# A decoder layer on one core: each weight unit ordered behind x's high part of the same rows, and the pre-norm's mean two rows later

## The chip, the cores and the metric

The kernel runs on one core of a Trainium2 chip. The metric is device microseconds of one launch; a kernel's time is the median of its runs.

## The reference

One decoder layer is applied to 288 tokens (256 of a prompt and 8 x 4 of a sample), with d_model 2048, d_ff 5632 and fp32 data:

```python
x = x + 0.5 * rmsnorm(swiglu(rmsnorm(x, g[0]), ffn1_w_in, ffn1_w_out), g[1])
m, sg, sh = hybrid_mixer(rmsnorm(x, g[2]), mix_w_in, ...)   # GLA heads and HGRN2 heads, with states
x = x + rmsnorm(m, g[3])
x = x + 0.5 * rmsnorm(swiglu(rmsnorm(x, g[4]), ffn2_w_in, ffn2_w_out), g[5])
```

`rmsnorm(x, w)` is `x * rsqrt(mean(x*x) + 1e-6) * w`. The layer's time lies in the products with the weights: `swiglu` has two, the mixer an input and an output projection.

## The kernel before

Activations are kept transposed: `x[k]` is a tile of 128 features (row k of 16, called a row below) by 288 tokens. The program goes through three stages: the first FFN, the mixer, the second FFN. Each starts with a pre-norm (`pre1`, `pre2`, `pre3`). The norm's factor per token, `rt`, is not put on x but on the results of the products, when they are taken out of PSUM; so the products can start before `rt` is known.

**Products in three parts.** A number is split into a high part in fp32r and the rest. For x that is `xh` (ScalarE, L272) and `xl` (VectorE, L273); for the weights `wh` (ScalarE, L101) and `wl` (VectorE, L102). A product is three matmuls: xh by wh (L550), xl by wh (L551), xh by wl (L552).

**Weight units.** The object `W` goes through the weights in units of 128 x 1024: two rows k, 2j and 2j+1, by 512 columns. SyncE loads them into `RAW_BUFS = 3` raw buffers (L74), 512 KB each, in order, so the load of unit i waits until `wl` of unit i-3 is done with its buffer. Split units lie in `HL_BUFS = 4` pairs of wh and wl; a pair is free when the matmuls of its unit are done. `W.ahead` splits units as far as there is room. If `W.behind` holds instructions, the next call of `ahead` orders its units behind them:

```python
            behind, self.behind = self.behind, None
            with ExitStack() as es:
                for ins in behind:
                    es.enter_context(self.tc.issue_after(ins))
                self.ahead(most)
            return
```

The order on each engine is set when the program is built, by a scheduler; `issue_after` gives it an instruction that has to stand earlier. On the chip each engine works through its list.

**Blocks.** `block(name, ...)` computes 512 output columns as four tiles of 128 features (`qk0_0` to `qk0_3`), over 16 rows. For each row it issues 12 matmuls and then calls `tick(k)`; after each unit it calls `W.ahead`. At the end each tile is taken out of its PSUM bank by `evac`. A stage's first two blocks are `gate1_0` and `up1_0` in stage 1, `qk0` and `v0` in stage 2, `gate2_0` and `up2_0` in stage 3. `tick0` of the pre-norm runs in the first block, `tick1` in the second.

**Between stages.** A post-norm's `update(k)` makes the new x of row k: y[k] times the post-norm's factor (L523), x[k] from it (L524), then xh[k] and xl[k]. Rows 0 to 7 are updated before the first block of stages 2 and 3 (`UPDATED = 8`), rows 8 to 15 by `tick0` in it, row k+8 at row k. For stage 1 `made` is given and x comes from the input. Some of row products of tile 0 are made ahead from the old x and y apart (`Fill`) and are added at the end of that tile: `fsum` L509 scales them, L512 adds them to the bank of `qk0_0`, which is free afterwards.

**The mean.** `tick1` squares x (ScalarE, L408) and adds the squares up in `acc` (VectorE, L412). At one row it calls `rstd`: a matmul of `acc` with a constant matrix (`pre`, L439), a square root on ScalarE (L179) and a reciprocal on VectorE (L441), which gives `rt`. Behind them come a few instructions on `gate` and the functions of `late`: in the mixer the scaling of q and k by `rt` (L1545) and the small weights `a32`; in stage 3 that of the gates by `rt` (L611). The first tiles of `v0` are multiplied by `rt` at L910 and L911. `a_lr` (L1555) is a small product of x with `a32`, scaled by `rt` at L1556 on VectorE, and its result goes into the matmuls `zp` (L1562), which stand some matmuls into the next block.

In stage 2 GpSimd also loads the recurrent states `s` (L1245), 256 KB each, while the first block runs.

## Time and profile before

| | us |
|---|---|
| median of 3 runs | 2261.44 |
| lowest, highest | 2260.63, 2262.22 |
| the profiled execution | 2260.56 |
| its span | 2258.8 |
| TensorE busy in it | 2244.1 |
| VectorE, ScalarE busy | 1361.7, 1005.1 |

The profile is of one execution. The span runs from its first to its last instruction; what the execution takes beyond it, 1.8 us, lies around it. Stage 2 begins near 860 us of the span, stage 3 near 1400. A row of a timeline gives start and duration, engine, line, operation, output and inputs by name without buffer numbers, and in brackets the idle time ahead with what ended it. Consecutive rows of one kind may be joined (x2), and matmuls overlap, so their starts are what counts.

### The profile page before, as it was taken

The numbers are of one execution on the slowest core, as the hardware profiler recorded it, in microseconds if no ns is written. First come the engines' busy times: TensorE is split into PE (matmuls) and PEld (weight loads), VectorE is DVE, ScalarE is ACT, GpSimd is POOL, SyncE is SP. The second block draws the span as 40 slices with busy tenths as digits, with TensorE's granted clock in tenths as the row PEclk, the third lists the DMA queues.
The fourth block names the chain that finished last, engine by engine and source line by source line (L and its number), as shares of the span: only waits on it lengthen the run. The fifth ranks groups of instructions, "written<-read, shape, count | busy, mean of one in ns | idle before, by whom it ended". The sixth has DMA issues, their size and how long they took to land. (4 is left out here: it accounts for less than half of the span.)

```text
span 2258.8 us, 41337 instructions
## 1 busy us (share of the span) xinstructions
PE 2244.1 (99%) x17073; PEld 2226.7 (99%) x17073; DVE 1361.7 (60%) x2164; ACT 1005.1 (44%) x1508; POOL 78.3 (3%) x143
## 2 busy tenths in 40 slices
PE   9999999999999999999999999999999999999998
PEld 9999999999999999999999999999999999999998
DVE  7545545554565468778888745744555455545554
ACT  6443333333334344545566644543333333333345
POOL 0000000000000003022110000100000000000000
PEclk9999999999999999999999999999999999999999
DMA  7555555555555555466565654555555555555553
GB/s 218 163 167 168 164 166 166 168 165 165 166 168 180 168 166 162 135 208 204 173 171 162 184 178 128 170 163 165 169 168 162 166 167 160 168 167 160 167 168 109
DMA packets 207107, 377.94 MB, mean 167 GB/s; under 512 B 15411, under 2 KB 40801, under 8 KB 206913
## 3 DMA queue, kind: packets, MB, share of 16 engines
q1 hardware_dynamic: 198608, 356.83, 52.3%
q0 software_dynamic: 5984, 17.97, 2.5%
q8 instruction: 135, 2.21, 0.4%
q10 hardware_dynamic: 2320, 0.44, 0.1%
q14 instruction: 60, 0.48, 0.1%
HBM read 363.39 MB, written 11.80 MB: 166 GB/s over the span
## 5 line engine op out<-in xcount | busy, mean ns | idle before, releaser
L102 DVE TENSOR_TENSOR wl<-raw,wh 128x1024 fp32r<-128x1024 f32 (+1 forms) x674 | 822.0, 1220 | 643.9 <-ACT wh L101 641.3
L101 ACT ACTIVATE wh<-raw 128x1024 fp32r<-128x1024 f32 (+1 forms) x673 | 710.6, 1057 | 1054.5 <-PE gate L551 313.2
L550 PE MATMUL gate<-xh,wh 128*128 128x288 f32 x1660 | 487.7, 297 | 0.0
L552 PE MATMUL gate<-xh,wl 128*128 128x288 f32 x1660 | 487.5, 295 | 0.0
L551 PE MATMUL gate<-xl,wh 128*128 128x288 f32 x1660 | 487.4, 295 | 0.0
L551 PE MATMUL out<-hl,wh 128*128 128x288 f32 x1408 | 415.9, 295 | 0.0
L550 PE MATMUL out<-hh,wh 128*128 128x288 f32 x1408 | 415.4, 295 | 0.0
L552 PE MATMUL up<-xh,wl 128*128 128x288 f32 x1408 | 415.2, 295 | 0.0
L552 PE MATMUL out<-hh,wl 128*128 128x288 f32 x1408 | 415.1, 295 | 0.0
L551 PE MATMUL up<-xl,wh 128*128 128x288 f32 x1408 | 415.0, 295 | 0.0
L550 PE MATMUL up<-xh,wh 128*128 128x288 f32 x1408 | 414.6, 294 | 0.0
L551 PEld LDWEIGHTS gate<-xl,wh 128*128 128x128 f32 x1660 | 311.5, 188 | 0.9 <-DVE xl L273 0.5
L552 PEld LDWEIGHTS gate<-xh,wl 128*128 128x128 f32 x1660 | 311.2, 188 | 0.0
L550 PEld LDWEIGHTS gate<-xh,wh 128*128 128x128 f32 x1660 | 310.2, 188 | 0.9 <-ACT xh L272 0.5
L552 PEld LDWEIGHTS out<-hh,wl 128*128 128x128 f32 x1408 | 264.8, 188 | 0.0
L550 PEld LDWEIGHTS out<-hh,wh 128*128 128x128 f32 x1408 | 264.7, 188 | 0.0
L551 PEld LDWEIGHTS out<-hl,wh 128*128 128x128 f32 x1408 | 264.6, 188 | 0.0
L552 PEld LDWEIGHTS up<-xh,wl 128*128 128x128 f32 x1408 | 264.3, 188 | 0.1
L551 PEld LDWEIGHTS up<-xl,wh 128*128 128x128 f32 x1408 | 264.2, 188 | 0.1
L550 PEld LDWEIGHTS up<-xh,wh 128*128 128x128 f32 x1408 | 264.2, 188 | 0.1
L680 DVE TENSOR_TENSOR y<-out,y 128x288 f32<-128x288 f32 x288 | 121.6, 453 | 104.1 <-PE out L552 101.3
L550 PE MATMUL hfq<-xh,wh 128*128 128x288 f32 x256 | 78.0, 305 | 0.0
(373 smaller groups left out, 2395.8 us busy)
## 6 DMA issues: line engine op xcount, KB each, us to landing
raw<-in_ffn_w_in_dram SPq DMA_DIRECT2D x351, 512.0 KB, 3.7
raw<-in_ffn_w_out_dram SPq DMA_DIRECT2D x176, 512.0 KB, 3.7
raw<-in_mix_w_in_dram SPq DMA_DIRECT2D x64, 512.0 KB, 3.7
raw<-in_mix_w_in_dram SPq DMA_DIRECT2D x96, 256.0 KB, 3.4
raw<-in_mix_w_out_dram SPq DMA_DIRECT2D x32, 512.0 KB, 3.7
out_dram<-s POOLq DMA_DIRECT2D x32, 256.0 KB, 3.4
s<-in_state_gla_dram POOLq DMA_DIRECT2D x16, 256.0 KB, 4.3
s<-in_state_hgrn_dram POOLq DMA_DIRECT2D x16, 256.0 KB, 4.7
```

Source lines behind the costliest of these rows:

```text
L101: i1 = self.nc.scalar.activation(h[:, c], raw[:, c], AF.Copy).ins
L102: i2 = self.nc.vector.tensor_tensor(l[:, c], raw[:, c], h[:, c].bitcast(F32), op=ALU.subtract).ins
L550: yield lambda: PE.matmul(dst, w[0][:, c:c + P], parts[0], start=start, stop=False)
L551: yield lambda: PE.matmul(dst, w[0][:, c:c + P], parts[1], start=False, stop=False)
L552: yield lambda: PE.matmul(dst, w[1][:, c:c + P], parts[0], start=False, stop=stop)
L680: V.tensor_tensor(y[k], ps, y[k], op=ALU.add)
```

## The change

In stages 2 and 3, where `made` is None, `tick0` hands `xh` of the row just updated to `W.behind`. The next `W.ahead`, one in two rows, then orders the units that it splits behind it: behind xh9, xh11, xh13 and xh15 at the latest rows of the pairs. And in all three stages `tick1` calls `rstd` with all that follows at row 11 instead of 9. The number of lines grows by two above L455, so L550 of before is L552 after.

```diff
         def tick0(self, k):
             if k + self.ahead < KT:
                 self.split = self.update(k + self.ahead)
+                if self.made is None:
+                    W.behind = self.split[:1]
 
         def tick1(self, k):
...
-            if k == 9:
+            if k == 11:
                 ins = rstd(rt, (acc,), self.name)
```

Each engine issues the same instructions as before; what moves is their order. Names carry the unit or row number, and behind an underscore a running number of the build.

ScalarE in stage 2, in the first block, from xh11 on; wh are the weight units, sq the squares. Before:

```order
L272 ACTIVATE xh11_141<-x11_109,prm_94 128x288
L101 ACTIVATE wh272_9487<-raw272_9359 128x1024
L272 ACTIVATE xh12_142<-x12_110,prm_94 128x288
L272 ACTIVATE xh13_143<-x13_111,prm_94 128x288
L101 ACTIVATE wh273_9517<-raw273_9391 128x1024
L272 ACTIVATE xh14_144<-x14_112,prm_94 128x288
L272 ACTIVATE xh15_145<-x15_113,prm_94 128x288
L408 ACTIVATE acc_164<-x0_98 128x288
L101 ACTIVATE wh274_9550<-raw274_9429 128x1024
L408 ACTIVATE sq_9618<-x1_99 128x288
```

And after:

```order
L272 ACTIVATE xh11_141<-x11_109,prm_94 128x288
L101 ACTIVATE wh270_9387<-raw270_9153 128x1024
L272 ACTIVATE xh12_142<-x12_110,prm_94 128x288
L272 ACTIVATE xh13_143<-x13_111,prm_94 128x288
L101 ACTIVATE wh271_9425<-raw271_9236 128x1024
L101 ACTIVATE wh272_9487<-raw272_9359 128x1024
L272 ACTIVATE xh14_144<-x14_112,prm_94 128x288
L101 ACTIVATE wh273_9517<-raw273_9391 128x1024
L272 ACTIVATE xh15_145<-x15_113,prm_94 128x288
L408 ACTIVATE acc_164<-x0_98 128x288
L408 ACTIVATE sq_9618<-x1_99 128x288
L408 ACTIVATE sq_9633<-x2_100 128x288
```

wh269 to wh271 have moved down by several rows behind xh9, xh11 and xh13 (before, they stood ahead of xh7). xh14 and xh15 were both behind wh273; now xh14 stands ahead of it, xh15 behind it, and wh274 comes after two squares.

VectorE at the same place: before, from y9 to wl270, the low half of the unit whose buffer raw273 is loaded into next.

```order
L523 TENSOR_TENSOR y9_123<-y9_123,post1s_9277 128x288
L102 TENSOR_TENSOR wl269_9356<-raw269_9122,wh269_9355 128x1024
L273 SCALAR_TENSOR_TENSOR xl7_153<-x7_105,prm_94,xh7_137 128x288
L273 SCALAR_TENSOR_TENSOR xl8_154<-x8_106,prm_94,xh8_138 128x288
L524 SCALAR_TENSOR_TENSOR x9_107<-y9_123,hg1_95,x9_107 128x288
L523 TENSOR_TENSOR y10_124<-y10_124,post1s_9277 128x288
L523 TENSOR_TENSOR y11_125<-y11_125,post1s_9277 128x288
L273 SCALAR_TENSOR_TENSOR xl9_155<-x9_107,prm_94,xh9_139 128x288
L524 SCALAR_TENSOR_TENSOR x10_108<-y10_124,hg1_95,x10_108 128x288
L524 SCALAR_TENSOR_TENSOR x11_109<-y11_125,hg1_95,x11_109 128x288
L102 TENSOR_TENSOR wl270_9388<-raw270_9153,wh270_9387 128x1024
```

And after, from wl269 to wl270:

```order
L102 TENSOR_TENSOR wl269_9356<-raw269_9122,wh269_9355 128x1024
L273 SCALAR_TENSOR_TENSOR xl10_156<-x10_108,prm_94,xh10_140 128x288
L526 SCALAR_TENSOR_TENSOR x11_109<-y11_125,hg1_95,x11_109 128x288
L525 TENSOR_TENSOR y12_126<-y12_126,post1s_9277 128x288
L525 TENSOR_TENSOR y13_127<-y13_127,post1s_9277 128x288
L273 SCALAR_TENSOR_TENSOR xl11_157<-x11_109,prm_94,xh11_141 128x288
L526 SCALAR_TENSOR_TENSOR x12_110<-y12_126,hg1_95,x12_110 128x288
L102 TENSOR_TENSOR wl270_9388<-raw270_9153,wh270_9387 128x1024
```

Between wl269 and wl270 stood eight rows and now six, but wl269 itself stands seven rows lower, so wl270 has xl10, xl11, y12, y13 and x12 ahead of it in addition. Further down on VectorE, wl274 stood between the two rows of `fsum` and now stands behind them.

TensorE and ScalarE at the mean of stage 2, in the block v0. TensorE before:

```order
L552 MATMUL v0_1_9602<-xh10_140,wl277_9682 128x288
L550 MATMUL v0_2_9603<-xh10_140,wh277_9681 128x288
L439 MATMUL pre2_9798<-acc_164,onesD_89 128x288
L551 MATMUL v0_2_9603<-xl10_156,wh277_9681 128x288
L552 MATMUL v0_2_9603<-xh10_140,wl277_9682 128x288
```

TensorE after:

```order
L553 MATMUL v0_3_9604<-xl11_157,wh277_9681 128x288
L554 MATMUL v0_3_9604<-xh11_141,wl277_9682 128x288
L439 MATMUL pre2_9829<-acc_164,onesD_89 128x288
L552 MATMUL v0_0_9601<-xh12_142,wh278_9724 128x288
L553 MATMUL v0_0_9601<-xl12_158,wh278_9724 128x288
```

The mean stood within row 10 and now stands between rows 11 and 12. ScalarE before:

```order
L408 ACTIVATE sq_9761<-x14_112 128x288
L408 ACTIVATE sq_9764<-x15_113 128x288
L101 ACTIVATE wh280_9854<-raw280_9685 128x1024
L179 ACTIVATE rt_162<-pre2_9798,epst_91 128x288
L172 ACT_TABLE_LOAD
```

ScalarE after:

```order
L408 ACTIVATE sq_9761<-x14_112 128x288
L101 ACTIVATE wh280_9798<-raw280_9685 128x1024
L408 ACTIVATE sq_9764<-x15_113 128x288
L101 ACTIVATE wh281_9885<-raw281_9728 128x1024
L179 ACTIVATE rt_162<-pre2_9829,epst_91 128x288
```

Here wh281 stood behind the square root and now stands ahead of it; on VectorE, wl281 stands ahead of the reciprocal in the same way, where wl280 was the last before it. In stage 3 ScalarE and VectorE move alike.

## The prediction

> **What bounds it.** I read the page first, then the waits of TensorE, then each wait in the timeline of the engines.

> ```profile
> span 2258.8 us, 41337 instructions
> ...
> PE 2244.1 (99%) x17073; PEld 2226.7 (99%) x17073; DVE 1361.7 (60%) x2164; ACT 1005.1 (44%) x1508; POOL 78.3 (3%) x143
> ...
> PEclk9999999999999999999999999999999999999999
> ```

> TensorE is busy for 2244.1 of 2258.8 us, and its clock stays in the top tenth. The change adds and drops no matmul, so all it can give is idle time: 14.7 us in the whole kernel. It touches three waits by name:

> ```profile
> PE qk L550 <- ACT xh L272: 1.6, 1, 1.6
> ...
> PE v L550 <- DVE fsum L512: 0.8, 1, 0.8
> ...
> PEld qk L551 <- DVE xl L273: 0.2, 1, 0.2
> ```

> and the waits of the pre-norm means on `acc`, shown below. The timeline of TensorE around the first two (start, duration, line, operation, idle before it and its releaser):

> ```profile
> 880.65 0.30 PE L551 MATMUL qk<-xl,wh 128*128 128x288 f32 x1
> 880.78 0.29 PE L552 MATMUL qk<-xh,wl 128*128 128x288 f32 x1
> 882.63 0.80 PE L550 MATMUL qk<-xh,wh 128*128 128x288 f32 x4 [1.56 <-ACT xh L272]
> ...
> 887.13 0.29 PE L552 MATMUL v<-xh,wl 128*128 128x288 f32 x1
> 888.18 0.40 PE L550 MATMUL v<-xh,wh 128*128 128x288 f32 x1 [0.76 <-DVE fsum L512]
> ```

> Matmuls start 0.13 us apart, so these two gaps lose 882.63 - 880.78 - 0.13 = 1.72 and 888.18 - 887.13 - 0.13 = 0.92. ScalarE and VectorE tell why:

> ```profile
> 881.10 1.06 ACT L101 ACTIVATE wh<-raw 128x1024 fp32r<-128x1024 f32 x1 [4.19 <-PE qk L552]
> 882.06 0.94 ACT L272 ACTIVATE xh<-x,prm 128x288 fp32r<-128x288 f32 x2
> ...
> 885.45 1.06 ACT L101 ACTIVATE wh<-raw 128x1024 fp32r<-128x1024 f32 x1 [2.11 <-DMA raw<-in_mix_w_in_dram]
> ```
> ```profile
> 886.54 1.23 DVE L102 TENSOR_TENSOR wl<-raw,wh 128x1024 fp32r<-128x1024 f32 x1 [1.48 <-ACT wh L101]
> 887.68 0.45 DVE L512 TENSOR_TENSOR fsum<-fsum,qk 128x288 f32<-128x288 f32 x1
> ```

> The row at 881.10 is wh273, at 882.06 xh14 and xh15, at 885.45 wh274. xh14 waited behind wh273, and the residual sum L512 behind wl274. For wh273 the profile names TensorE, but the DMA came last:

> ```profile
> L74 SPq DMA_DIRECT2D raw<-in_mix_w_in_dram x1: 367/367/367, 874.0 to 874.0; - x1
> DMA to landing us min/median/max: 7.0/7.0/7.0
> ...
> L74 SPq DMA_DIRECT2D raw<-in_mix_w_in_dram x1: 368/368/368, 877.6 to 877.6; - x1
> DMA to landing us min/median/max: 7.8/7.8/7.8
> ```
> ```profile
> L1245 POOL DMA_DIRECT2D s<-in_state_gla_dram x7: 704/716/727, 871.4 to 875.7; - x7
> DMA to landing us min/median/max: 3.3/5.5/8.6
> ```
> ```profile
> 876.00:882.00 6.00, 5.07 (x39) 4.84 (x37) 5.26 (x9) 1.81 (x3) 6.00 (x22) 1.00 0.93 314
> ```
> ```profile
> raw<-in_ffn_w_in_dram SPq DMA_DIRECT2D x5, 512.0 KB, 3.6
> ```

> raw273 (issued 874.0) took 7.0 us and raw274 7.8, among seven state loads of 256 KB; the row of 876 to 882 (length, busy us of PE, PEld, DVE, ACT and POOL, PE clock, DMA share, GB/s) has the DMA engines 93% busy at 314 GB/s. The same loads at the third stage's start, without state loads (last row), take 3.6.

> **The change, step by step: stage 2 (mixer).** ScalarE used to take wh269 to wh273 as their buffers allowed; now they stand behind xh9, xh11, xh13 (two) and xh14. VectorE's wl units follow, and each raw load waits for the wl three units earlier, so loads go out later:

> ```profile
> 870.66 0.81 DVE L523 TENSOR_TENSOR y<-y,post1s 128x288 f32<-128x288 f32 x2
> ...
> 871.82 0.94 DVE L524 SCALAR_TENSOR_TENSOR x<-y,hg,x 128x288 f32<-128x288 f32 x2
> 872.68 1.22 DVE L102 TENSOR_TENSOR wl<-raw,wh 128x1024 fp32r<-128x1024 f32 x1
> 873.81 0.94 DVE L273 SCALAR_TENSOR_TENSOR xl<-x,prm,xh 128x288 fp32r<-128x288 f32 x2
> ```

> wl270 (872.68) now has xl10, xl11, y12, y13 and x12 ahead of it as well: two L523 (0.8), three of 0.43 (1.3), together 2.1. So raw273 is issued at about 876.1 instead of 874.0. Its landing L is the unknown: 876.1 + 3.6 = 879.7 if the engines are free, 876.1 + 7.8 = 883.9 if it fares as raw274. I take 881.8, the middle, and a count of bytes gives the same: the loads up to raw273 are those of before, landed by 881.0, except that about 0.25 MB of raw272 used to move before the state loads began; that is 0.8 us at 314 GB/s.

> Now xh14 no longer stands behind wh273, but xh15 does. TensorE would come to xh15 seven matmuls after xh14, at 880.78 + 8 x 0.13 = 881.8. Before, landing to resumption took 882.63 - 881.0 = 1.6 (wh273, then the xh), and does again: TensorE resumes at L + 1.6. The old waits (1.72 + 0.92, and 0.2 for the low half xl7, which wl269 used to hold up) give 2.84; the second cannot return as it was, since the sum L512 now stands ahead of wl274. The gain is Q = 2.84 - (L + 1.6 - 881.6) = 882.8 - L, hence **1.0** at 881.8, between -1.1 (883.9) and, if nothing waits, 2.84.

> **The later mean.** Before, TensorE waited for the last `acc`:

> ```profile
> 903.39 0.29 PE L550 MATMUL v<-xh,wh 128*128 128x288 f32 x1
> 904.32 0.72 PE L439 MATMUL pre<-acc,onesD 128*128 128x288 f32 x2 [0.63 <-DVE acc L412]
> 904.67 0.51 PE L551 MATMUL v<-xl,wh 128*128 128x288 f32 x1
> ...
> 1440.67 0.72 PE L439 MATMUL pre<-acc,onesD 128*128 128x288 f32 x2 [0.47 <-DVE acc L412]
> ```
> ```profile
> 54.03 0.29 PE L552 MATMUL up<-xh,wl 128*128 128x288 f32 x1
> ...
> 54.67 0.38 PE L550 MATMUL up<-xh,wh 128*128 128x288 f32 x1
> ```

> Stages 2 and 3 lose 0.63 and 0.47; stage 1 passes its mean in 54.67 - 54.03 = 0.64 with no wait. Behind row 11 the mean comes 17 matmuls later in stage 2 and 20 in stage 3, over 2 us, so both waits go: **-0.63, -0.47**. But everything on `rt` comes later too, and in stage 2 a consumer was just in time:

> ```profile
> 905.65 1.95 DVE L441 RECIPROCAL rt<-rt 128x288 f32<-128x288 f32 x1
> ...
> 909.70 1.23 DVE L102 TENSOR_TENSOR wl<-raw,wh 128x1024 fp32r<-128x1024 f32 x1
> ...
> 911.30 0.42 DVE L910 TENSOR_TENSOR y<-v,rt 128x256 f32<-128x256 f32 x1 [0.26 <-PE v L552]
> ...
> 915.87 0.45 DVE L1556 TENSOR_TENSOR y<-a_lr,rt 128x288 f32<-128x288 f32 x1
> ```
> ```profile
> 913.59 2.15 PE L1555 MATMUL a_lr<-x,a 128*32 128x288 f32 x32
> ...
> 916.42 1.19 PE L1562 MATMUL zp<-y,y 128*128 128x288 f32 x4
> ```

> Let E be the end of row 11 on TensorE. ScalarE now has wh281 ahead of the square root (0.96) and VectorE wl281 behind it, ahead of the reciprocal (1.13): with 0.15 for handing over, the reciprocal starts at E + 2.25. From it to L1556 went 915.87 - 905.65 = 10.2; wl281 (1.13) and the idle 0.26 drop out, two short instructions on `lb` come in (0.2): 9.0. With 0.55 from L1556 to zp, zp can start at E + 11.8. TensorE gets there after the mean (0.64), rows 12 to 15 (48 x 0.133 = 6.4) and the stretch from a_lr to zp (916.42 - 913.59 = 2.8): E + 9.9. This is a new wait of **+1.9** at zp, where none stood. Its bounds: 0 if VectorE's chain has slack that I don't see, 3.0 if it holds one wl unit (1.13) more than counted. Stage 2 sums to -1.0 - 0.63 + 1.9 = +0.3.

> **Stage 3 and stage 1.** In stage 3 ScalarE and VectorE move in the same way, but a load takes 3.6 us, so wh417 is not late: I take -0.47 for the mean and -0.2 for the low half behind the early weight unit (as in stage 2), with 0 to +0.6 for banks that are freed later because `rt` is (half of the wl unit of 1.13 that now stands ahead of the reciprocal). Consumers of `rt` there, as in stage 1, are evacuations after the whole row 15; the order moves the first matmuls of the block that reuses the bank six places back, which covers 0.8 of it. Stage 1 gets no new weight order: 0, at most +0.6.

> **Sum**: +0.3 - 0.7 + 0 = -0.4 us against the profiled execution's 2260.56, that is 2260.2. The runs' median, 2261.44, lies 0.9 above it: **2261.0**.

> [...]

> **Rivals.**
> - *All removed waits pay.* raw273 lands by 880.2 and zp does not wait: 2.84 + 0.63 + 0.47 + 0.2 = 4.1 less, 2257.3. For it: the load asks for what others no longer need at 880. Against it: 93% busy engines, and the VectorE row above. Chance 0.07.
> - *The load comes late, slower.* raw273 is now asked for in the thick of the state loads, and xh15 stands behind it. At L = 883.9 Q is -1.1, and the sum +1.7: 2263.1. It makes the kernel slower from L = 882.2 on, and by 0.2% only from 887. For it: 7.8 for the neighbour, 8.6 for a state load. Chance 0.2.
> - *rt too late everywhere.* If banks in stages 1 and 3 wait too, 0.6 each by the bound above: 2262.2. It speaks for it that zp had no slack, against it that evacuations there follow row 15. Chance 0.17.
> - *The clock drops.* A gap at xh15 (L + 1.6 less 881.6, so 3.9 us at 883.9) makes TensorE idle long enough that some matmuls run slower: at half the clock for as long as the gap, 2 us more, 2265.1. Against it: the gap of 1.85 from 880.78 left the clock of 876 to 882 at 1.00, in the row of that stretch. Chance 0.03. [...]

> **Numbers.** My forecast has 0.53. About 0.2% (4.5 us) is what a measurement can tell from no change here. Of all cases only the first with something on top ends faster by that (0.03), and the late load or the clock with another loss slower (0.04); 0.93 stays within. The range runs from 2258.5, with Q at 2.84 and two thirds of the zp wait, to 2263.4, just beyond the late load.

> **What would show it.** TensorE's waits should no longer list fsum L512 nor acc L412 at the means; a wait of qk on xh L272 of 1 to 3 us should stand at xh15 near 883, with wh L101 released by the DMA ahead of it; a wait of zp L1564 on y L1558 (new line numbers) of about 2 us should be new near 917. No wait at zp, or none at xh15, would each prove its step wrong. A total beyond 2266 would mean a wait in stages 1 or 3 that I have not seen, or a lower clock.

## The result and the profile after

The changed kernel is slower: 2266.93 us (median of 14 runs, 2263.96 to 2268.80) against 2262.59 for the kernel before in the same sets of runs (14 runs, 2260.57 to 2265.28). The ratio is 1.0018, 95% interval 1.0011 to 1.0026, so 4.3 us. That is just inside the 0.2% to which the chances were given, but on the other side than forecast, and beyond the range's upper end of 2263.4. Two launches among the runs below, 2710.38 us of the weight order alone and 2408.93 us of the kernel with 24 filling matmuls, had a granted clock of 0.75 and 0.85 and are left out of the ratios.

The waits of TensorE in the changed kernel's profile (line, releaser, us in total, times, longest):

```profile
PE qk L552 <- ACT xh L272: 3.4, 1, 3.4
...
PE zp L1564 <- DVE y L1558: 1.4, 1, 1.4
PE sc L1356 <- DVE Qv L1311: 0.9, 2, 0.6
PE pre L439 <- DVE acc L412: 0.3, 1, 0.3
```

The wait on fsum is gone, the means' waits have shrunk to 0.3, and zp waits anew, all as forecast. But the wait on xh has grown from 1.6 to 3.4. TensorE's timeline at that place, and behind it the stretches of 4 us from 880 to 896 (length, busy us and count of PE, PEld, DVE, ACT, POOL, PE clock, DMA share, GB/s):

```profile
883.29 0.30 PE L553 MATMUL qk<-xl,wh 128*128 128x288 f32 x1
883.43 0.29 PE L554 MATMUL qk<-xh,wl 128*128 128x288 f32 x1
887.07 0.85 PE L552 MATMUL qk<-xh,wh 128*128 128x288 f32 x2 [3.35 <-ACT xh L272]
887.72 0.44 PE L553 MATMUL qk<-xl,wh 128*128 128x288 f32 x1
887.96 0.44 PE L554 MATMUL qk<-xh,wl 128*128 128x288 f32 x1
```
```profile
880.00:884.00 4.00, 3.72 (x29) 3.48 (x27) 3.96 (x6) 1.74 (x3) 4.00 (x13) 1.00 1.01 333
884.00:888.00 4.00, 0.93 (x4) 0.93 (x5) 0.95 (x2) 2.46 (x6) 4.00 (x10) 0.71 0.81 249
888.00:892.00 4.00, 4.00 (x18) 4.00 (x18) 2.71 (x5) 1.60 (x3) 2.48 (x7) 0.50 0.55 147
892.00:896.00 4.00, 4.00 (x30) 4.00 (x30) 2.76 (x6) 0.74 (x2) 0.00 (x0) 0.94 0.52 144
```
```profile
882.25:885.66 3.41, 1.47 (x12) 1.23 (x10) 1.71 (x3) 0.12 (x1) 3.41 (x9) 1.00 0.98 296
885.67:892.48 6.81, 5.41 (x22) 5.41 (x23) 4.14 (x8) 4.36 (x7) 4.81 (x12) 0.50 0.57 169
```

Behind the gap matmuls start 0.24 apart instead of 0.13, and the granted clock is 0.50: 18 matmuls in 4 us where 30 are usual. The last two rows show the edges: the recorded clock is 1.00 up to 885.66 and 0.50 from there to 892.49. 21 steps of 0.24 in a row, each 0.107 too long, cost 2.2 us. Busy time counts them as work: TensorE's grew from 2244.1 to 2248.3 us.

ScalarE and the load of raw273 show whose wait it was:

```profile
881.23 0.52 ACT L272 ACTIVATE xh<-x,prm 128x288 fp32r<-128x288 f32 x1
885.54 1.06 ACT L101 ACTIVATE wh<-raw 128x1024 fp32r<-128x1024 f32 x1 [3.79 <-DMA raw<-in_mix_w_in_dram]
886.50 0.52 ACT L272 ACTIVATE xh<-x,prm 128x288 fp32r<-128x288 f32 x1
```
```profile
L74 SPq DMA_DIRECT2D raw<-in_mix_w_in_dram x1: 368/368/368, 878.0 to 878.0; - x1
...
DMA to landing us min/median/max: 7.4/7.4/7.4
```

The load of wh273 was issued at 878.0 and took 7.4 us; xh15 stood behind it.

To compare kernels, the same matmul is looked up in both traces and its start is subtracted; the table gives how the median difference to the first profile of the kernel before grows over each stretch (positive is slower; times are those of the kernel before). "Opening" is 855 to 895, "mean" to 908, "zp" to 925, "rest of mixer" to 1300, "stage 3" from 1398 to 1456.

| kernel | opening | mean | zp | rest of mixer | stage 3 |
|---|---|---|---|---|---|
| before, again | -0.2 | 0.0 | 0.0 | +0.4 | 0.0 |
| changed | +3.0 | -0.4 | +1.6 | +0.4 | -0.2 |
| changed, again | +3.3 | -0.4 | +3.6 | +1.8 | -0.7 |
| weight order alone | +2.3 | -0.1 | +1.2 | +0.3 | +0.5 |
| mean at row 11 alone | -0.2 | -0.9 | +2.1 | +0.7 | -0.4 |
| mean at row 10 alone | +0.8 | -0.7 | 0.0 | +0.2 | -0.7 |
| mean at row 10 alone, again | +0.7 | -0.7 | 0.0 | +0.4 | -0.7 |
| 24 filling matmuls | +2.4 | -0.9 | +3.6 | +1.4 | -0.7 |
| 12 filling matmuls | +1.3 | -0.9 | +2.1 | +3.0 | -0.7 |
| small state loads | -2.3 | -0.4 | +1.7 | +5.1 | -0.7 |
| units past xh15, mean at 10 | -1.6 | -0.4 | +1.1 | -0.1 | -0.2 |
| one unit held, mean at 10 | 0.0 | -0.7 | 0.0 | +0.1 | -0.7 |
| one held behind the sum too | -2.9 | +0.3 | +1.0 | +1.1 | -0.7 |

Ahead of the opening no kernel differs but by the start of the program: in the first profile of before the clock came up early, and most later profiles lost 1.5 to 2.2 us there, the changed kernel's among them (the last section shows it). Of the span's growth from 2258.8 to 2265.2, 2.2 us are of that kind and not the change's; the stretches of the changed kernel sum to +4.4.

### The profile page after: what moved, and what is told of

It reads as the page before. It is cut to its first block, busy times and chain, and to the rows that moved or that the text cites. A ratio compares the mean times of both kernels' runs of the same rounds, so it can differ in the third digit from the quotient of the medians.

```text
span 2265.2 us, 41340 instructions
## 1 busy us (share of the span) xinstructions
PE 2248.3 (99%) x17073; PEld 2230.4 (98%) x17073; DVE 1361.4 (60%) x2164; ACT 1006.6 (44%) x1508; POOL 77.1 (3%) x143
## 5 line engine op out<-in xcount | busy, mean ns | idle before, releaser
L102 DVE TENSOR_TENSOR wl<-raw,wh 128x1024 fp32r<-128x1024 f32 (+1 forms) x674 | 821.5, 1220 | 646.5 <-ACT wh L101 644.3
L101 ACT ACTIVATE wh<-raw 128x1024 fp32r<-128x1024 f32 (+1 forms) x673 | 710.6, 1057 | 1047.4 <-PE gate L553 311.1
L552 PE MATMUL gate<-xh,wh 128*128 128x288 f32 x1660 | 489.3, 297 | 0.2 <-ACT xh L272 0.2
L552 PE MATMUL out<-hh,wh 128*128 128x288 f32 x1408 | 415.4, 295 | 0.0
L552 PE MATMUL up<-xh,wh 128*128 128x288 f32 x1408 | 414.5, 295 | 0.0
L552 PEld LDWEIGHTS gate<-xh,wh 128*128 128x128 f32 x1660 | 310.9, 188 | 1.7 <-ACT xh L272 0.9
L552 PEld LDWEIGHTS out<-hh,wh 128*128 128x128 f32 x1408 | 264.6, 188 | 0.1
L552 PEld LDWEIGHTS up<-xh,wh 128*128 128x128 f32 x1408 | 264.0, 188 | 0.2
L552 PE MATMUL hfq<-xh,wh 128*128 128x288 f32 x256 | 78.0, 305 | 0.0
## 6 DMA issues: line engine op xcount, KB each, us to landing
raw<-in_ffn_w_in_dram SPq DMA_DIRECT2D x351, 512.0 KB, 3.7
raw<-in_ffn_w_out_dram SPq DMA_DIRECT2D x176, 512.0 KB, 3.7
raw<-in_mix_w_in_dram SPq DMA_DIRECT2D x64, 512.0 KB, 3.8
raw<-in_mix_w_out_dram SPq DMA_DIRECT2D x32, 512.0 KB, 3.7
```

The source lines that it names most:

```text
L101: i1 = self.nc.scalar.activation(h[:, c], raw[:, c], AF.Copy).ins
L102: i2 = self.nc.vector.tensor_tensor(l[:, c], raw[:, c], h[:, c].bitcast(F32), op=ALU.subtract).ins
L552: yield lambda: PE.matmul(dst, w[0][:, c:c + P], parts[0], start=start, stop=False)
```

## The experiments

**The two parts apart.** The weight order alone (`k == 11` back to `k == 9`), and the mean alone:

```diff
-                if self.made is None:
-                    W.behind = self.split[:1]
```

> The weight units stand behind xh in stages 2 and 3, the mean stays at row 9. Theory A (the late raw273 and the clock): TensorE idles for over 3 us at xh15 as in the changed kernel, and the granted clock of 888 to 892 is 0.50; with 0.9 for the longer gap and 2.4 for the slow matmuls the kernel is slower than before by about 3 us, and zp does not wait. Theory B (the later rt is what costs, the gap is made up for by the waits that went): within 1 us of before.

> The mean at row 11, weight units ordered as before. Theory A: zp waits for 1.4 to 2 us, the waits on acc at the means (1.1) are gone, so 0 to 1 us slower than before; the clock stays at 1.00 in stage 2. Theory B: 3 to 4 us slower than before.

The weight order alone took 2265.03 us against 2262.14 (11 and 33 runs), ratio 1.0015 (1.0005 to 1.0024): 2.9 slower, as theory A said. It has the gap and the low clock:

```profile
885.37 0.53 PE L552 MATMUL qk<-xh,wh 128*128 128x288 f32 x2 [3.61 <-ACT xh L272]
```
```profile
884.00:888.00 4.00, 2.63 (x13) 2.63 (x14) 2.02 (x3) 3.27 (x6) 4.00 (x10) 0.76 0.49 152
888.00:892.00 4.00, 4.00 (x27) 4.00 (x26) 3.93 (x7) 1.06 (x1) 0.53 (x2) 0.81 0.63 164
886.10:889.50 3.40, 3.40 (x16) 3.40 (x15) 2.69 (x5) 1.59 (x3) 2.43 (x7) 0.50 0.48 122
```

Two points went against the expectation. The low clock was shorter than in the changed kernel, 3.41 us with 14 slow matmuls, so 1.5 us and not 2.4. And zp waited here too, for 1.0, with `k == 9` as before. The trace shows why: the new weight order moves the mean as well. Between it and zp stand 88 of TensorE's instructions instead of 103, so TensorE comes to zp sooner behind the mean by 15 x 0.133 = 2.0 us, while y, for which zp waits, begins only 0.7 sooner behind it (10.86 us instead of 11.55).

The mean alone took 2262.64 against 2262.14, ratio 1.0006 (0.9997 to 1.0015): no difference that can be told, which is theory A's 0 to 1. In its profile the waits on acc are gone and zp waits in their place:

```profile
884.10 0.80 PE L550 MATMUL qk<-xh,wh 128*128 128x288 f32 x4 [2.23 <-ACT xh L272]
...
918.17 1.24 PE L1562 MATMUL zp<-y,y 128*128 128x288 f32 x4 [1.88 <-DVE y L1556]
```

So about 2.9 of the 4.3 are the weight order's (its interval is 1.1 to 5.4), most of it in the opening of stage 2 (+2.3). The two parts alone sum to 3.4; what is missing to 4.3 is within the intervals.

**Is it the clock?** Matmuls on xh0 into a bank that nobody reads, between xh14's and xh15's in qk0; first 24, then 12:

```diff
+                if name == "qk0" and f == 0 and k == KT - 1:
+                    held = self_ins[-1]
+                    with tc.issue_after(held):
+                        dum = auxtile("dum")
+                        for _ in range(FILL):
+                            held = PE.matmul(dum[:, 0:T], xh[0][:, 0:P], xh[0], start=True, stop=True).ins
+                    with tc.issue_after(held):
+                        mm(ws[k // per - (nu - tail)], f, k)
```

> The changed kernel with 24 matmuls added between xh14's and xh15's in the block qk0, into a bank that nobody reads: 24 x 0.133 = 3.2 us of TensorE work where it idled for 3.5. Theory A with the clock: TensorE goes on at the same time as in the changed kernel, the clock stays at 1.00, and 2.4 us are won against the changed kernel. Rival (the slow matmuls after the gap have another cause, such as operands that come late): no time won, the matmuls after the gap start 0.24 apart as before.

With 24, the first half came as expected: TensorE went on when xh15 was there, and the clock stayed at 1.00.

```profile
882.74 3.32 PE L594 MATMUL dum<-xh 128*128 128x288 f32 x24
886.32 0.40 PE L554 MATMUL qk<-xh,wh 128*128 128x288 f32 x1 [0.26 <-ACT xh L273]
...
890.81 0.40 PE L554 MATMUL v<-xh,wh 128*128 128x288 f32 x1 [0.87 <-DVE fsum L515]
```
```profile
884.00:888.00 4.00, 3.59 (x25) 3.14 (x24) 1.70 (x3) 3.22 (x6) 4.00 (x9) 1.00 0.67 198
888.00:892.00 4.00, 3.13 (x23) 2.77 (x21) 3.90 (x10) 2.05 (x4) 2.43 (x6) 1.00 0.67 157
```

But the time was not won: 2267.66, ratio 1.0024 (1.0014 to 1.0033). In this build wl274 stands ahead of the residual sum again, so the wait on fsum was back. And the clock fell later instead: behind a wait of 1.89 at zp it was 0.50 from 922.6 to 926.1, with 14 slow matmuls, 1.5 of the 3.6 in the zp column. A second try with 12 leaves the order of wl274 and the sum as in the changed kernel.

> The changed kernel with 12 idle-time matmuls instead of 24 ahead of xh15's; VectorE's order of the residual sum ahead of wl274 is that of the changed kernel this time. They fill 1.6 us of the gap, so TensorE idles for about 2 us. Theory A with the clock: a gap of 2.2 left the clock at 1.00 with the mean alone, so this one does too, the opening of stage 2 (up to 895 us) is 2 to 2.4 us shorter than in the changed kernel, and so is the whole. Rival (the clock goes down for any gap behind so many late rows, or the slow matmuls cost nothing because what follows is waiting anyway): no more than 0.5 us won.

```profile
886.51 0.40 PE L554 MATMUL qk<-xh,wh 128*128 128x288 f32 x1 [1.82 <-ACT xh L273]
```
```profile
884.00:888.00 4.00, 2.02 (x14) 1.58 (x13) 1.51 (x2) 3.02 (x6) 4.00 (x10) 1.00 0.75 227
888.00:892.00 4.00, 4.00 (x30) 3.81 (x30) 4.00 (x10) 1.92 (x3) 2.42 (x6) 1.00 0.68 161
```

The clock stayed up, and the opening cost +1.3 instead of +3.0 and +3.3: 1.7 to 2.0 us won where 2 to 2.4 were expected. The whole was 2266.63 (ratio 1.0020, 1.0011 to 1.0029), no faster than the changed kernel, because +3.0 came in the rest of the mixer near 1108. Half of it is a gap of 1.5 in which TensorE waited for Qv of VectorE; the other half is the clock again, which fell behind that gap:

```profile
1111.10:1114.50 3.40, 3.40 (x14) 3.40 (x15) 2.47 (x7) 0.54 (x2) 0.00 (x0) 0.50 0.11 14
```

The clock's share is thus shown in its stretch, not in the whole.

**Why raw273 is late.** The changed kernel with an eighth of the state bytes:

```diff
-                        G.dma_start(t, s0[b0:b0 + nb, a].rearrange("b p v -> p b v"))
+                        G.memset(t, 0.0)
+                        G.dma_start(t[0:16], s0[b0:b0 + nb, a, 0:16].rearrange("b p v -> p b v"))
```

> The changed kernel, but each state load brings 16 of its 128 partitions and the rest is set to zero, so the sample's states are wrong; the state loads move an eighth of their bytes. Theory A: raw273 lands within 4.5 us of its issue, so xh15 waits for less than 1 us, the clock stays at 1.00, and against the changed kernel about 5 us are won (gap 3 and clock 2.4), against before about 1. Rival (the load is late for its late issue alone, not for the state loads): the landing takes over 6 us, and less than 1 us is won.

```profile
L74 SPq DMA_DIRECT2D raw<-in_mix_w_in_dram x1: 368/368/368, 876.3 to 876.3; - x1
...
DMA to landing us min/median/max: 4.3/4.3/4.3
```
```profile
882.31 0.54 PE L552 MATMUL qk<-xh,wh 128*128 128x288 f32 x2 [0.27 <-ACT xh L272]
```

raw273 now takes 4.3 us, xh15 waits for 0.27, the clock stays up, and the opening is 5.2 us better than in the changed kernel (-2.3 against +3.0): the state loads make the load late. The whole, 2264.83 against 2262.14 (ratio 1.0015, 1.0006 to 1.0024), hides it, since 5 us were lost near 1265 in a place that this edit brought about:

```profile
PE gate L552 <- DVE z L1635: 2.7, 2, 1.5
```
```profile
1265.00:1270.00 5.00, 2.26 (x14) 1.79 (x13) 5.00 (x11) 3.37 (x6) 0.00 (x0) 0.96 0.44 116
1270.00:1275.00 5.00, 5.00 (x30) 5.00 (x29) 2.74 (x6) 2.21 (x5) 0.00 (x0) 0.70 0.65 199
```

Why those waits came there was not followed further.

**Is it the late load, or what stands behind it?** The changed kernel with xh15 in force for the units of rows 9 and 11 too, and the mean at row 10:

```diff
                 if self.made is None:
                     W.behind = self.split[:1]
+            elif self.made is None and k < 12:
+                W.behind = self.split[:1]
```

> The changed kernel, but the last xh (row 15) stays in force for the units that rows 9 and 11 split, so wh272 and wh273 stand behind xh15, and the mean is at row 10. raw273 still lands near 884. Theory A (what costs is xh15 behind the late unit): no wait at xh15, clock at 1.00, at most 1.5 us of waiting at row 2 of v0 for wh273; zp waits for less than 0.7; in all 0 to 2 us faster than before. Rival (the late load costs wherever its unit stands): a gap of about 2 us moves to row 2 of v0, and the kernel is 1 to 2 us slower than before.

2261.84 against 2262.50, ratio 0.9997 (0.9988 to 1.0006). xh15 no longer waits, row 2 of v0 waits for wl273 for 0.7, the opening is 1.6 better than before:

```profile
L74 SPq DMA_DIRECT2D raw<-in_mix_w_in_dram x1: 367/367/367, 877.4 to 877.4; - x1
...
DMA to landing us min/median/max: 7.2/7.2/7.2
```
```profile
887.15 0.40 PE L556 MATMUL v<-xh,wl 128*128 128x288 f32 x1 [0.70 <-DVE wl L102]
```

raw273 lands at 884.6, less the 1.6 that this trace runs late 883.0, nearly as late as in the changed kernel (883.3). With only its own unit behind it, the late load costs that wait of 0.7, and the clock stays up. zp waited for 0.9, more than expected; here 89 instructions stand between the mean and zp, against 98 with the mean at row 10 alone.

**The kernel before with one unit held**, only wh273 behind xh15, and the mean at row 10; then also wl274 behind the residual sum (its `W.ahead` moved behind the sum, with `W.behind` on the addition):

```diff
+            elif self.made is None and k in (11,):
+                W.behind = self.split[:1]
...
-            if k == 9:
+            if k == 10:
```

> The kernel before with one unit held: only the unit that row 11 splits (wh273, and its fellow in stage 3) is ordered behind xh15; the others stay early, and the mean is at row 10. raw273 is asked for at 874 and lands at 881 as before, and xh14 and xh15 no longer wait for it. Theory A: the gap of 1.7 at xh14 goes, the waits on acc (1.1) go, the wait on fsum (0.9) stays, zp waits for less than 0.5: 2 to 3 us faster than before. Rival (the cover is elsewhere, another wait takes their place): within 1 us of before.

2261.97, ratio 0.9997 (0.9988 to 1.0006): the expectation of 2 to 3 us missed. The wait at xh14 went, and the wait on fsum grew from 0.8 to 2.0: wl274 is as late as before, and TensorE came to it sooner.

```profile
888.32 0.40 PE L552 MATMUL v<-xh,wh 128*128 128x288 f32 x1 [1.97 <-DVE fsum L514]
```

> The kernel with one held unit and the mean at row 10, and besides the unit that used to stand ahead of the residual sum on VectorE (wl274, and its fellow in stage 3) ordered behind that sum. Theory A: the wait of 2.0 on fsum that took the place of the wait at xh14 goes too, TensorE waits for less than 1 us in all between 864 and 918, and the kernel is 2.5 to 4 us faster than before. Rival (wl274 comes so late that row 4 of v0 waits for it): within 1 us of before.

2260.88 against 2262.35, ratio 0.9995 (0.9986 to 1.0004): again missed. The opening is 2.9 us shorter, all of 1.72 + 0.92 + 0.2. What follows gives most of it back:

```profile
905.32 0.72 PE L439 MATMUL pre<-acc,onesD 128*128 128x288 f32 x2 [0.96 <-DVE acc L412]
...
916.64 1.24 PE L1567 MATMUL zp<-y,y 128*128 128x288 f32 x4 [0.76 <-DVE y L1561]
```
```profile
PE sc L1359 <- DVE Qv L1314: 1.4, 2, 0.8
```

Each of these waits ends with VectorE. Its row for 864 to 880, in the kernel before and in this one, shows that it has no time left there:

```profile
864.00:880.00 16.00, 16.00 (x122) 15.84 (x121) 15.88 (x35) 8.31 (x14) 8.56 (x22) 1.00 0.51 158
```
```profile
864.00:880.00 16.00, 16.00 (x121) 15.86 (x121) 15.88 (x34) 9.06 (x15) 6.76 (x15) 1.00 0.43 126
```

VectorE is busy for 15.88 of 16 us. Its share of 60% over the whole kernel does not show that. That the waits come back because VectorE cannot follow is argued from this row, not shown: from 888 to 904 it is busy for 12.9 of 16 us in this kernel, and the order moved too (90 of TensorE's instructions from the mean to zp, against 98 with the mean at row 10 alone).

**The mean at row 10 alone**, twice:

> The kernel before with the mean at row 10 and nothing else. The reciprocal keeps its place ahead of wl281. Theory A: waits on acc (1.1) gone, zp waits for at most 0.5, 0.5 to 1 us faster than before, which is at the edge of what can be measured. Rival (each row that the mean moves costs as much at zp as it wins): no change.

> The mean at row 10 once more. In its first profile a gap of 1.94 at xh14 was followed by slow matmuls (granted clock 0.73 and 0.84 in 884 to 892), where a gap of 2.23 with the mean at row 11 was not. Theory A (the clock looks at stretches that lie where they lie, so a gap near 2 us sometimes costs it and sometimes not): the gap is again 1.5 to 2.3, and the clock may be 1.00 this time. Rival (the order of this kernel brings it each time): 0.7 to 0.85 again.

2260.95 against 2262.50 (11 and 33 runs), ratio 0.9992 (0.9983 to 1.0001). The waits on acc are gone and zp does not wait: -0.7 at each mean, as expected, at the edge of what can be told. No version here beats the kernel before clearly. In both profiles the gap at xh14 was followed by a lower clock (rows of 884 to 888, the first profile's and the second's):

```profile
884.73 0.80 PE L550 MATMUL qk<-xh,wh 128*128 128x288 f32 x4 [1.94 <-ACT xh L272]
```
```profile
884.00:888.00 4.00, 3.27 (x17) 3.27 (x18) 3.29 (x5) 3.17 (x7) 4.00 (x9) 0.73 0.60 169
```
```profile
884.31 0.81 PE L550 MATMUL qk<-xh,wh 128*128 128x288 f32 x4 [1.77 <-ACT xh L272]
```
```profile
884.00:888.00 4.00, 3.69 (x17) 3.69 (x18) 2.45 (x4) 1.89 (x4) 4.00 (x9) 0.62 0.65 170
```

**Both kernels once more**, for the clock:

> The changed kernel once more, for the wait at xh15 and the clock behind it. Theory A: a gap of 3.2 to 3.7 us at xh15 and a granted clock of 0.5 for 3 to 5 us behind it, as in its first profile. Rival (the first profile was an accident of that execution): no slow matmuls.

> The kernel before once more. Theory A: a gap of 1.5 to 2.3 at xh14, its length set by raw273's landing, and a clock of 1.00 or somewhat below behind it; the opening of stage 2 differs from its first profile by no more than 2.5 us.

The changed kernel (2269.79 us in this one execution) had a gap of 3.60 at xh15 and a clock of 0.50 from 888 to 892 again, and slow matmuls behind its wait of 1.75 at zp as well. The kernel before (2262.35) had a gap of 1.71 at xh14 and a clock of 1.00. The first profile of the changed kernel was no accident.

## Why the prediction was wrong

- **That the three old waits go** was right: fsum and xl7 are gone and the waits on acc shrank from 1.1 to 0.3.
- **The issue of raw273** was right: forecast at 876.1. It was 878.0 in a trace that ran 2.2 late at that point, so 875.9.
- **The landing L = 881.8 was the first step that failed.** It was 885.4, less 2.2 so 883.3, near the bound of 883.9. The count of bytes assumed that the same bytes land at the same time. Instead raw273, with the full state loads, took 7.0 us from its own issue in the kernel before, 7.4 in the changed one and 7.2 with the units past xh15, whether it was issued at 874.0 or 1.9 later. raw274's 7.8 was the better row for the likeliest value and not only for an end. Not every load in that traffic was so slow: the changed kernel's raw272 and raw274 took 4.8 each, and why they differ stays open. By the prediction's own formula Q was then 882.8 - 883.3 = -0.5, not +1.0. With it the sum is +1.1 instead of -0.4, that is 2262.5: slower, but still inside the range.
- **The slow matmuls behind the gap were the second and the larger: 2.2 us for which the sum had nothing.** The low clock was a rival with 0.03, priced at 2 us more for a gap of 3.9. The gap was 3.5 (887.07 - 883.43 - 0.13), the price 2.2. Half the clock for as long as the gap was my estimate, and no row of before showed it behind a gap; in the changed kernel's trace the clock was 0.50 for 6.83 us, 1.41 of them still in the gap and 5.42 behind it. The row I held against it could exclude nothing: its gap was half as long, and it ended at 882.00, before TensorE went on at 882.63. The chance of the low clock also hung on the chance of the late landing (0.2), which makes 0.03 too little. Both rivals came together: the formula's -0.5 and the clock make 2.7 of the opening's 3.0, and 2262.5 + 2.2 = 2264.7 is outside the range. What is left to 2266.93 is 0.3 in the opening, 0.4 in the rest of the mixer, 0.5 in stage 3, and 1.15 by which the kernel before itself ran longer in these sets than the 2261.44 I started from (to rounding).
- **The wait at zp**: +1.9 forecast, 1.38 measured, and 1.88 with the mean alone. The row by row sum was good. Missed was that the weight order by itself brings a wait there (1.0), since it moves the mean 15 of TensorE's instructions nearer to zp.
- **Stage 3**: -0.7 forecast, -0.2 and -0.7 in two profiles. The mean wins 0.4 to 0.7 there, the weight order loses (+0.5 alone). Stage 1 is within 0.2, as forecast.
- **The direction** fell with L: -0.4 was a small difference of gains and a wait that were each several times as large, and the one unknown moved it by a bound of 4 us. The clock then made the change large enough to be told from none.

In the runs three of three gaps of 3.35 to 3.61 us were followed by a granted clock of 0.50, and so were five single gaps of 1.50 to 1.94; the last section goes into it.

## What to carry to other kernels

When a queue of one engine mixes urgent small work with units that wait for a transfer, look at what stands behind the unit in the queue: the same late load cost a gap of 3.5 us and 2.2 us of slow matmuls with xh15 behind it, and a wait of 0.7 with xh15 ahead. Take the landing of a delayed transfer from rows of the same traffic (raw273's own 7.0 and raw274's 7.8, for the 7.4 measured) and not from the middle between these and a load that is alone (3.6). Price an idle gap on TensorE with the slow matmuls behind it: here nine falls of the granted clock to 0.50 cost 0.6 to 2.4 us each, behind gaps of 1.50 to 3.61 us. Look also at how busy the engines are in that stretch alone before removing a wait: here VectorE had 99% in it, and waits of 1.72 and 0.92 that were removed came back in large part at the next places that needed VectorE.

## What was not expected of the hardware

In these traces the clock did not go by the length of one gap. Ten gaps of 1.7 to 2.3 us were seen inside the program; four were followed by matmuls 0.24 apart (1.94 and 1.77 at xh14 with the mean at row 10, 1.75 at zp in the changed kernel's second profile, 1.89 at zp with 24 filling matmuls), six were not (2.23 and 1.88 with the mean at row 11 alone, 1.97 with one unit held, 1.82 and 1.9 with 12 filling matmuls, 1.71 in the second profile of the kernel before). Two gaps of 1.54 and 1.20 with three matmuls between them cost 15 slow steps near 1270, with the small state loads.

The start of the program has the same spread. From 8 to 11 us TensorE ran 23 matmuls in the first profile of the kernel before and 14 in its second:

```profile
8.00:11.00 3.00, 3.00 (x23) 3.00 (x22) 1.77 (x4) 1.63 (x4) 0.00 (x0) 1.00 1.05 351
```
```profile
8.00:11.00 3.00, 3.00 (x14) 2.98 (x14) 1.75 (x4) 1.13 (x3) 0.00 (x0) 1.00 1.04 328
```

The 1.00 in these two rows says nothing: the record of the clock begins at 8.70 us in the first and at 11.52 us in the second, and the view prints 1.00 where there is no record. Ahead of its beginning most matmuls start 0.24 apart, behind it 0.13. Over the fourteen profiles the beginning lies between 8.70 and 12.12 us, and by and large the later it lies, the later the program is: 11.52 instead of 8.70 is 2.82 us at half pace, which would lose 1.4, and 1.5 were lost; in the changed kernel it is 11.85, and 2.2 were lost.
